# A diagonal state-space scan beside an RWKV-7 recurrence: its state tiles one by one, or in pairs side by side in the rows and columns of TensorE's array

## The chip, the core and the metric

The kernel runs on one core of a Trainium2 chip. The metric is the device time of one execution in microseconds (us). The kernel before takes 1673.89 us, the median of three runs (1672.61 to 1677.13).

## What is computed

Two layers of an encoder trunk on 256 tokens of width 1024, in float32. The even layer projects the normed tokens to two mixers, RWKV-7 time mixing (8 heads of 64) and an S5 diagonal complex state-space model (32 groups of 16 channels, 64 complex states each), and projects both outputs back; then come cross-attention to a memory of 256 tokens and a dense SwiGLU. The odd layer has differential attention, cross-attention to the same memory and 8 SwiGLU experts, two for each token. The change is in the S5 model:

```python
def s5_ssm(u, lam_re, lam_im, log_dt, b_re, b_im, c_re, c_im, d_skip, w_glu, b_glu):
    ug = u.reshape(b, t, S5_GROUPS, S5_GROUP)
    lam_bar = jnp.exp(lam * dt)
    b_bar = ((lam_bar - 1.0) / lam)[..., None] * lax.complex(b_re, b_im)
    bu = jnp.einsum('gpi,btgi->btgp', b_bar, ug)          # inputs of the states
    _, states = lax.associative_scan(combine, (lam_bar, bu), axis=1)   # x[t] = lam_bar * x[t-1] + bu[t]
    y = jnp.real(jnp.einsum('gip,btgp->btgi', c_mat, states))
    y = jax.nn.gelu(y + d_skip * ug)
    return y * jax.nn.sigmoid(y @ w_glu + b_glu)
```

## The kernel before

The 32 groups with 64 states each make 2048 complex states, which are worked on in 16 **state tiles** of 128 states on the partitions and 256 tokens along the free axis, real and imaginary part side by side (128 x 2 x 256). Tile j belongs to channel block m = j // 4 (128 channels) and to the 32 channels q = j % 4 of that block. A tile goes through three steps, which are functions in `s5_scan` (lines 546 to 609):

- `inputs(j)`: two float32 matmuls make the tile `pbu` in PSUM, one for each part. They contract over 32 channels only, so they use 32 rows of TensorE's array (rows 32q to 32q+31) and all 128 columns. VectorE multiplies `pbu` with a cosine into `xc` (L561) and with a sine into `zz` (L562), and GpSimd (POOL) adds the products (L563, L564): the states are turned by a phase table, after which the recurrence is real.
- `scan(j)`: VectorE runs the recurrence with two scan instructions (L569), one for each part, and the result is turned back: a product on VectorE (L571), one on VectorE or, for every second tile, on POOL (L574), and two POOL additions (L575, L576).
- `outputs(j)`: two matmuls that contract over the 128 states and give 32 channels, so they use all rows and 32 columns of the array (columns 32q to 32q+31). Four tiles fill one PSUM tile `py` of 128 channels; then `gelu(m)` follows.

The phase tables `tbl` (`s5_table`, lines 401 to 420) hold four tiles each; the pool has two, so tables 2 and 3 are made on the way. The pool `s5w` holds two `xc`, two `zz` and two `t1`; `ps_tr` holds two `pbu`.

The work around it: the projections of the even layer (`feat_linear`, `project`; their weights are split into two rounded halves, `wh` on ScalarE and `wl` on VectorE, L178 and L184, and multiplied in three passes, L190 to L192) from the start to 132 us; then the RWKV-7 block matrices, states and outputs (`block_matrices`, `block_states`, `block_output`: many 32x32 and 64x64 matmuls `pm`, `po`, with VectorE steps `qq`, `w`, `vt` between them), the S5 gate and the output projection. In all of this the keys and values of the memory for both layers (`memory_kv`, tiles `pf`, weights `fraw`, split on ScalarE L450 and VectorE L453) are the **filler** of TensorE. `chain()` and `pipeline()` (lines 1000 to 1044) emit the steps: each generator yields a TensorE cost and a latency, and filler goes between. The S5 tiles begin in the projections: the scheduler, which simulates the engines and takes what is ready by priority, fixes the order on each engine. Weights of this stage come through a ring of three `raw` tiles (`weight_pools(cx, 3, 2, 2)`, line 755). All loads are issued in order by one queue (SP), `raw` (L173) and `fraw` (L440) alike.

## Time and profile before

| what | value |
|---|---|
| median of three runs | 1673.89 us (1672.61 to 1677.13) |
| profiled execution | 1672.61 us, span from first to last instruction 1670.8 us |
| TensorE (PE) busy | 1619.4 us, 97% of the span |
| VectorE (DVE) busy | 639.9 us, 38% |
| ScalarE (ACT), GpSimd (POOL) busy | 476.1 us (28%), 198.5 us (12%) |
| mean granted TensorE clock | 0.976 |
| chain that ended last | PE 86%, DVE 8%, ACT 2%, POOL 2%, issue 2% |

The shares are means over stages that differ. VectorE's 38% is the mean of a first fifth in which it is busy most of the time and a rest in which it is nearly idle; the change touches that first fifth only. A granted clock of 1.00 is 2.4 GHz, 0.50 is 1.2 GHz.

### The profile page before, as it was taken

The numbers are of one execution on the slowest core, as the hardware profiler recorded it, in microseconds if no ns is written. First come the engines' busy times: TensorE is split into PE (matmuls) and PEld (weight loads), VectorE is DVE, ScalarE is ACT, GpSimd is POOL, SyncE is SP. The second block draws the span as 40 slices with busy tenths as digits, with TensorE's granted clock in tenths as the row PEclk, the third lists the DMA queues.
The fourth block names the chain that finished last, engine by engine and source line by source line (L and its number), as shares of the span: only waits on it lengthen the run. The fifth ranks groups of instructions, "written<-read, shape, count | busy, mean of one in ns | idle before, by whom it ended". The sixth has DMA issues, their size and how long they took to land.

```text
span 1670.8 us, 34308 instructions
## 1 busy us (share of the span) xinstructions
PE 1619.4 (97%) x14882; PEld 982.9 (59%) x14882; DVE 639.9 (38%) x1065; ACT 476.1 (28%) x852; POOL 198.5 (12%) x230
## 2 busy tenths in 40 slices
PE   6999999999999999999999999999999999999997
PEld 5877657899999988998334333343333433333432
DVE  7778987676555567764100011100101001010011
ACT  6466434555544456653101000010000100010000
POOL 6334473111000031110000000000000000000000
PEclk9999979999999999998999999999999999999999
DMA  6423323664555543646699889999999999999995
GB/s 227 152 89 127 109 71 115 222 255 152 186 193 180 195 156 116 239 150 239 252 387 383 333 356 407 415 418 419 419 418 418 419 419 419 418 419 387 372 419 218
DMA packets 74462, 471.48 MB, mean 282 GB/s; under 512 B 8600, under 2 KB 10008, under 8 KB 22464
## 3 DMA queue, kind: packets, MB, share of 16 engines
q1 hardware_dynamic: 73024, 465.02, 71.5%
q0 software_dynamic: 1280, 4.20, 0.7%
q8 instruction: 118, 1.93, 0.5%
q14 instruction: 40, 0.33, 0.1%
HBM read 463.94 MB, written 5.24 MB: 281 GB/s over the span
## 4 chain that ended last, share of the span: by engine, by line
PE 86%; DVE 8%; ACT 2%; POOL 2%; issue 2%; DMA 0%; SPq 0%; DVEq 0%; POOLq 0%; ACTq 0%
PE pgu L195 31%; PE pd L195 16%; PE pm L190 5%; PE pm L192 5%; PE pm L191 5%; PE pgu L190 2%; PE pgu L192 2%; PE pgu L191 2%; PE pm L195 2%; PE pgt L195 1%; PE pf L190 1%; PE pf L191 1%; PE pf L192 1%; PE po L195 1%; DVE zz L569 1%
## 5 line engine op out<-in xcount | busy, mean ns | idle before, releaser
L195 PE MATMUL pgu<-raw,gx 128*32 128x512 f32 (+1 forms) x5376 | 515.8, 542 | 0.0
L195 PEld LDWEIGHTS pgu<-raw,gx 128*32 128x32 f32 x5376 | 171.9, 110 | 319.8 <-issue 287.2
L195 PE MATMUL pd<-raw,th 128*32 128x512 f32 x2352 | 266.4, 607 | 0.4 <-DVE th L1896 0.4
L184 DVE TENSOR_TENSOR wl<-raw,wh 128x1024 fp32r<-128x1024 f32 (+1 forms) x159 | 195.0, 1238 | 103.2 <-ACT wh L178 102.8
L178 ACT ACTIVATE wh<-raw 128x1024 fp32r<-128x1024 f32 (+1 forms) x160 | 165.5, 1047 | 146.8 <-PE pgu L191 67.7
L1882 DVE SCALAR_TENSOR_TENSOR actA<-pgu,gs,actA 128x512 f32<-128x512 f32 (+1 forms) x32 | 21.9, 684 | 468.0 <-PE pgu L195 282.7
L195 PEld LDWEIGHTS pd<-raw,th 128*32 128x32 f32 x2352 | 75.5, 112 | 175.2 <-issue 171.7
L190 PE MATMUL pm<-xh,wh 128*128 128x256 f32 (+1 forms) x552 | 161.6, 296 | 14.4 <-ACT wh L178 12.4
L192 PE MATMUL pm<-xh,wl 128*128 128x256 f32 (+1 forms) x552 | 158.0, 290 | 4.9 <-DVE wl L184 4.9
L191 PE MATMUL pm<-xl,wh 128*128 128x256 f32 (+1 forms) x552 | 159.0, 289 | 2.2 <-DVE xl L1096 2.2
L1878 ACT ACTIVATE actA<-pgu,gs 128x512 f32<-128x512 f32 (+1 forms) x32 | 20.3, 634 | 448.5 <-PE pgu L195 433.5
L190 PEld LDWEIGHTS pm<-xh,wh 128*128 128x128 f32 (+1 forms) x552 | 107.6, 196 | 17.5 <-ACT wh L178 12.9
L192 PEld LDWEIGHTS pm<-xh,wl 128*128 128x128 f32 (+1 forms) x552 | 106.7, 195 | 7.1 <-DVE wl L184 6.4
L191 PEld LDWEIGHTS pm<-xl,wh 128*128 128x128 f32 (+1 forms) x552 | 107.8, 195 | 3.7 <-DVE xl L1096 2.6
L1896 DVE COPY th<-ptA 128x384 f32<-128x384 f32 (+3 forms) x32 | 14.9, 464 | 245.0 <-PE ptA L1895 245.0
L191 PE MATMUL pgu<-xl,wh 128*128 128x256 f32 x352 | 98.6, 280 | 0.0
L190 PE MATMUL pgu<-xh,wh 128*128 128x256 f32 x352 | 98.5, 280 | 0.0
L192 PE MATMUL pgu<-xh,wl 128*128 128x256 f32 x352 | 98.5, 280 | 0.0
L192 PEld LDWEIGHTS pgu<-xh,wl 128*128 128x128 f32 x352 | 66.2, 188 | 0.0
L191 PEld LDWEIGHTS pgu<-xl,wh 128*128 128x128 f32 x352 | 66.2, 188 | 0.0
L190 PEld LDWEIGHTS pgu<-xh,wh 128*128 128x128 f32 x352 | 66.1, 188 | 0.0
L453 DVE SCALAR_TENSOR_TENSOR fwl<-fraw,cols,fwh 128x512 fp32r<-128x512 f32 x64 | 56.9, 896 | 11.4 <-ACT fwh L450 11.3
(477 smaller groups left out, 2138.9 us busy)
## 6 DMA issues: line engine op xcount, KB each, us to landing
raw<-mg SPq DMA_DIRECT2D x112, 1024.0 KB, 15.5
raw<-mu SPq DMA_DIRECT2D x112, 1024.0 KB, 15.3
raw<-md SPq DMA_DIRECT2D x112, 1024.0 KB, 14.9
raw<-wgu SPq DMA_DIRECT2D x22, 1024.0 KB, 4.9
fraw<-wkv SPq DMA_DIRECT2D x32, 512.0 KB, 4.1
raw<-wqkv SPq DMA_DIRECT2D x12, 1024.0 KB, 4.9
raw<-wdn SPq DMA_DIRECT2D x11, 1024.0 KB, 4.9
raw<-hy SPq DMA_DIRECT2D x16, 512.0 KB, 3.8
```

What stands on the lines that cost most here:

```text
L178: W["act"].append(nc.scalar.activation(wh, rv, AF.Copy).ins)
L184: W["dve"].append(e_.tensor_tensor(wl[:, c_], rv[:, c_], wh[:, c_], op=ALU.subtract).ins)
L190: nc.tensor.matmul(out, lhsT=lt[0], rhs=r[0], start=start, stop=False, **kw)
L191: nc.tensor.matmul(out, lhsT=lt[0], rhs=r[1], start=False, stop=False, **kw)
L192: nc.tensor.matmul(out, lhsT=lt[1], rhs=r[0], start=False, stop=stop, **kw)
L195: nc.tensor.matmul(out, lhsT=lt, rhs=r, start=start, stop=stop, **kw)
L453: e_.scalar_tensor_tensor(wl, rv, g, wh, op0=ALU.mult, op1=ALU.subtract)
L569: nc.vector.tensor_tensor_scan(z[:, ri], rho[:, j:j + 1].to_broadcast([128, T]), xc[:, ri], 0.0, op0=ALU.mult, op1=ALU.add)
L1878: nc.scalar.activation(actA, p[0], AF.Silu, scale=gs[:, 0, 1:2])
L1882: nc.vector.scalar_tensor_tensor(actA, p[1], gs[:, 0, 1:2], actA, op0=ALU.mult, op1=ALU.mult)
L1896: nc.vector.tensor_copy(th[:, 0], ptA[:, :, 0:c])
```

## The change

The 16 state tiles become 8 pairs J = 0 to 7 (tiles 2J and 2J+1). `inputs(J)` makes both `pbu` of a pair, and its four matmuls alternate between the two tiles, which lie in different rows of the array. `outputs(J)` does the same in different columns. In the loop the scan of pair J-1 now stands ahead of the inputs of pair J, and a step is charged 1.6 us and twice the latency. The `xc` tiles move to a pool of four, `t1` to a pool of its own that is opened after the projections, and the ring of weight tiles of that stage shrinks from three to two, which pays for the room. The arithmetic is the same: as many matmuls, VectorE and POOL instructions as before.

```diff
@@ pools of the hybrid layer (line 231)
     s5t = scoped(cx, "s5t", 2)
     s5w = scoped(cx, "s5w", 2)
+    s5x = scoped(cx, "s5x", 4)
     s5 = scoped(cx, "s5", 1)
@@ s5_scan (line 546)
-        def inputs(j):
-            m, q = j // 4, j % 4
-            rows = slice(32 * q, 32 * q + 32)
-            sc = tables[m][:, q]
-            pbu = ps_tr.tile([128, 2, T], F32, name="pbu", tag="tr")
+        def inputs(J):
+            m = J // 2
+            pbu = [ps_tr.tile([128, 2, T], F32, name="pbu", tag="tr") for _ in range(2)]
             for ri in range(2):
-                mm(pbu[:, ri], sbw[rows, ri, m], uT[rows, m])
-            xc = xs[j] = s5w.tile([128, 2, T], F32, name="xc", tag="xc")
-            z = zs[j] = s5w.tile([128, 2, T], F32, name="zz", tag="zz")
-            nc.vector.tensor_tensor(xc, pbu, bc2(sc[:, 0]), op=ALU.mult)
-            nc.vector.tensor_tensor(z, pbu, bc2(sc[:, 1]), op=ALU.mult)
-            gtt(xc[:, 0], xc[:, 0], z[:, 1], op=ALU.add)
-            gtt(xc[:, 1], xc[:, 1], z[:, 0], op=ALU.subtract)
+                for i in range(2):
+                    q = 2 * (J % 2) + i
+                    rows = slice(32 * q, 32 * q + 32)
+                    mm(pbu[i][:, ri], sbw[rows, ri, m], uT[rows, m])
+            for i in range(2):
+                j = 2 * J + i
+                sc = tables[m][:, j % 4]
+                xc = xs[j] = s5x.tile([128, 2, T], F32, name="xc", tag="xc")
+                z = zs[j] = s5w.tile([128, 2, T], F32, name="zz", tag="zz")
+                nc.vector.tensor_tensor(xc, pbu[i], bc2(sc[:, 0]), op=ALU.mult)
+                nc.vector.tensor_tensor(z, pbu[i], bc2(sc[:, 1]), op=ALU.mult)
+                gtt(xc[:, 0], xc[:, 0], z[:, 1], op=ALU.add)
+                gtt(xc[:, 1], xc[:, 1], z[:, 0], op=ALU.subtract)
-        def scan(j):
+        def scan(J):
+            for j in (2 * J, 2 * J + 1):
...
-        def outputs(j):
-            m, q = j // 4, j % 4
-            if q == 0:
+        def outputs(J):
+            m = J // 2
+            if J % 2 == 0:
                 pys[m] = ps_po.tile([128, T], F32, name="py", tag="po")
-            terms = ((0, xs[j][:, 0]), (1, xs[j][:, 1]), (1, zs[j][:, 0]), (0, zs[j][:, 1]))[:4 if S5N else 2]
-            for i, (c, x) in enumerate(terms):
-                mm(pys[m][32 * q:32 * q + 32], cpad[:, c, j], x, i == 0, i == len(terms) - 1)
+            for c in range(2):
+                for i in range(2):
+                    q = 2 * (J % 2) + i
+                    mm(pys[m][32 * q:32 * q + 32], cpad[:, c, 2 * J + i], xs[2 * J + i][:, c], c == 0, c == 1)
...
-            t1 = s5w.tile([128, T], F32, name="t1", tag="t1")
+            t1 = s5g.tile([128, T], F32, name="t1", tag="t1")
...
-        for j in range(18):
-            if j > 1:
-                outputs(j - 2)
-            if j < 16:
-                inputs(j)
-            if 0 < j < 17:
-                scan(j - 1)
-            yield 1.3, S5_LAT
-            if j > 4 and j % 4 == 1:
-                gelu((j - 2) // 4)
-            if j in (5, 9):
-                s5_table(2 + j // 8)
+        for J in range(10):
+            if J > 1:
+                outputs(J - 2)
+            if 0 < J < 9:
+                scan(J - 1)
+            if J < 8:
+                inputs(J)
+            yield 1.6, 2 * S5_LAT
+            if J > 2 and J % 2:
+                gelu((J - 3) // 2)
+            if J in (2, 4):
+                s5_table(1 + J // 2)
@@ pools after the projections (line 751)
     ps_po = scoped(cx, "ps_po", 1, space=PSUM)
+    s5g = scoped(cx, "s5g", 2)
     ub = scoped(cx, "ub", 2)
-    weight_pools(cx, 3, 2, 2)
+    weight_pools(cx, 2, 2, 2)
@@ s5_gate (line 956)
-            t1 = s5w.tile([128, T], F32, name="t1", tag="t1")
+            t1 = s5g.tile([128, T], F32, name="t1", tag="t1")
```

The order on the engines at three places follows. Numbers behind a name tell buffers apart: `py_1639<-xc_1525` is an output product of the first tile. Lines of the changed kernel are a few higher than those of before (the scan is L569 before and L577 now; the products of the inputs are L561, L562 before and L568, L569 now).

TensorE at the end of the projections (132 us in the trace of before). Before:

```order
L195 MATMUL py_1639<-xc_1525,cpad_307 32x256 x2
L195 MATMUL py_1639<-xc_1576,cpad_307 32x256 x2
L764 MATMUL pt_1219<-cst_64,v_1179 128x128
L764 MATMUL pt_1225<-cst_64,v_1179 128x128
L764 MATMUL pt_1232<-cst_64,kt_1026 128x128 x4
L764 MATMUL pt_1219<-cst_64,v_1179 128x128
L764 MATMUL pt_1225<-cst_64,v_1179 128x128
L195 MATMUL pbu_1815<-uT_175,sbw_308 128x256 x2
L764 MATMUL pt_1238<-cst_64,kt_1026 128x128 x4
L195 MATMUL pbu_1902<-uT_175,sbw_308 128x256 x2
```

and now (the four output products of pair 0, in the same order, stand ahead of these):

```order
L195 MATMUL py_1708<-xc_1628,cpad_310 32x256
L195 MATMUL py_1708<-xc_1634,cpad_310 32x256
L195 MATMUL py_1708<-xc_1628,cpad_310 32x256
L195 MATMUL py_1708<-xc_1634,cpad_310 32x256
L770 MATMUL pt_1225<-cst_64,v_1182 128x128
L770 MATMUL pt_1231<-cst_64,v_1182 128x128
L770 MATMUL pt_1238<-cst_64,kt_1029 128x128 x4
L770 MATMUL pt_1225<-cst_64,v_1182 128x128
L770 MATMUL pt_1231<-cst_64,v_1182 128x128
L195 MATMUL pbu_1880<-uT_178,sbw_311 128x256 x2
L770 MATMUL pt_1244<-cst_64,kt_1029 128x128 x4
L195 MATMUL pbu_1881<-uT_178,sbw_311 128x256 x2
```

Before, the outputs of tiles 0 and 1 stand here, two matmuls of one tile and then two of the other, and the inputs of tiles 4 and 5, each alone. Now the outputs of four tiles stand here, alternating in pairs, and the inputs of pair 3 (tiles 6 and 7), which transposes keep apart.

TensorE among the 32x32 blocks of the RWKV-7 recurrence. Before (tile 8) and now (pair 6):

```order
L195 MATMUL pm_2483<-w_1725,aa_1429 32x32 x13
L195 MATMUL py_2462<-xc_2217,cpad_307 32x256
L195 MATMUL pm_2483<-w_1725,aa_1429 32x32 x8
L195 MATMUL py_2462<-xc_2217,cpad_307 32x256
L195 MATMUL pm_2483<-w_1725,aa_1429 32x32 x11
L195 MATMUL pm_2524<-w_1767,aa_1470 32x32 x32
```

```order
L195 MATMUL py_2604<-xc_2323,cpad_310 32x256
L195 MATMUL pm_2628<-w_1797,aa_1476 32x32 x25
L195 MATMUL py_2604<-xc_2329,cpad_310 32x256
L195 MATMUL py_2604<-xc_2323,cpad_310 32x256
L195 MATMUL pm_2628<-w_1797,aa_1476 32x32 x7
L195 MATMUL pm_2674<-qq_1748,vt_1747 32x32 x7
L195 MATMUL py_2604<-xc_2329,cpad_310 32x256
L195 MATMUL pm_2674<-qq_1748,vt_1747 32x32 x25
```

Both kernels have output products here one by one between the small blocks. Of pair 6 the middle two, one of each tile, stand together.

VectorE around `zm`, the result of the low-rank projection (51.9 us in the trace of before). Before, and now:

```order
L571 TENSOR_TENSOR xc<-zz,tbl 128x512
L569 SCALAR_TENSOR_TENSOR zz<-s5c_302,xc 128x256 x2
L474 TENSOR_SCALAR mem<-mem,rs 128x1024
L574 TENSOR_TENSOR zz<-zz,tbl 128x512
L571 TENSOR_TENSOR xc<-zz,tbl 128x512
L184 TENSOR_TENSOR wl<-raw,wh 128x1024
L617 TENSOR_TENSOR zm<-pm,rsB_149 128x2x256
L618 TENSOR_TENSOR zm<-pm,rsB_149 32x256
```

```order
L577 SCALAR_TENSOR_TENSOR zz<-s5c_305,xc 128x256 x2
L568 TENSOR_TENSOR xc<-pbu,tbl 128x512
L577 SCALAR_TENSOR_TENSOR zz<-s5c_305,xc 128x256 x2
L568 TENSOR_TENSOR xc<-pbu,tbl 128x512
L579 TENSOR_TENSOR xc<-zz,tbl 128x512 x2
L184 TENSOR_TENSOR wl<-raw,wh 128x1024
L581 TENSOR_TENSOR zz<-zz,tbl 128x512
L622 TENSOR_TENSOR zm<-pm,rsB_152 128x2x256
L623 TENSOR_TENSOR zm<-pm,rsB_152 32x256
```

Ahead of `zm` there are now two more products `xc<-pbu` (L568), those of pair 1; the products `zz<-pbu` and the scans of pair 1, and the third phase table, follow behind `zm`, in the projections, where before they stood behind the last projection.

## Rows read from the trace of the kernel before

**Rows 1.** The page of the whole execution: its first line, the and the busy time of each engine.
```profile
span 1670.8 us, 34308 instructions
...
PE 1619.4 (97%) x14882; PEld 982.9 (59%) x14882; DVE 639.9 (38%) x1065; ACT 476.1 (28%) x852; POOL 198.5 (12%) x230
```

**Rows 2.** Busy time of each engine by stage, from the first input product to the end of the output projection. Columns: stretch in us, its length, busy us and instructions of PE, PEld, DVE, ACT and POOL, granted TensorE clock, DMA share, GB/s.
```profile
37.00:60.00 23.00, 20.44 (x141) 17.72 (x140) 21.11 (x32) 9.65 (x16) 16.26 (x20) 0.93 0.44 138
60.00:100.00 40.00, 40.00 (x248) 33.54 (x247) 22.01 (x33) 23.55 (x44) 5.95 (x8) 1.00 0.47 152
100.00:135.00 35.00, 31.40 (x189) 26.13 (x188) 28.11 (x38) 18.64 (x42) 11.20 (x9) 0.90 0.35 116
135.00:224.00 89.00, 85.25 (x1485) 57.19 (x1483) 82.96 (x138) 44.02 (x73) 44.97 (x48) 0.98 0.34 107
224.00:241.30 17.30, 16.41 (x291) 9.99 (x291) 15.56 (x25) 6.26 (x16) 13.92 (x18) 0.51 0.05 19
241.30:270.00 28.70, 26.21 (x221) 17.34 (x220) 20.95 (x29) 11.05 (x24) 17.72 (x18) 0.94 0.35 120
270.00:345.00 75.00, 75.00 (x556) 66.61 (x554) 53.75 (x84) 41.93 (x67) 14.77 (x20) 1.00 0.57 207
```

**Rows 3.** The chain that ended last, of the stretch 132 to 262 us alone, by engine and line.
```profile
by line: DVE zz L569 12.3%; issue 11.2%; DVE fwl L453 9.8%; DVE zz L562 5.2%; PE pm L195 5.0%; DVE xc L571 4.8%; PE py L195 4.3%; DVE xc L561 4.3%; POOL xc L564 3.4%; POOL xc L576 2.7%; DVE wl L184 2.6%; POOL xc L563 2.6%; PE pf L190 2.6%; 
```

**Rows 4.** TensorE's instructions in order of time: start in us, from the first start to the last end, line, tiles, shapes, how many of one kind stand together (a float32 matmul is two instructions), and the idle time ahead with what ended it. First two input products together and what comes next, at 38 us.
```profile
37.91 1.14 PE L195 MATMUL pbu<-uT,sbw 32*128 32x256 f32 x8
38.98 0.31 PE L190 MATMUL pm<-xh,wh 128*32 128x256 f32 x1
```

**Rows 5.** The same view from 131 to 150 us: output products of two tiles, input products of one tile, two products of the same tile apart or of two tiles together.
```profile
132.00 1.06 PE L195 MATMUL py<-xc,cpad 128*32 128x256 f32 x8
133.00 0.44 PE L764 MATMUL pt<-cst,v 128*128 128x128 f32 x2
...
134.43 1.13 PE L195 MATMUL pbu<-uT,sbw 32*128 32x256 f32 x4 [0.34 <-DVE zz L562]
135.49 0.66 PE L764 MATMUL pt<-cst,kt 128*128 128x128 f32 x4
...
148.08 0.62 PE L195 MATMUL py<-xc,cpad 128*32 128x256 f32 x2
148.63 0.74 PE L190 MATMUL pf<-fwh,mth 128*128 128x512 f32 x2
149.29 0.63 PE L195 MATMUL py<-xc,cpad 128*32 128x256 f32 x4
149.85 0.34 PE L195 MATMUL pm<-bt,ar 64*64 64x64 f32 x4
```

**Rows 6.** The same view at 182 us (both products of one tile) and at 230 us (single products).
```profile
182.02 1.05 PE L195 MATMUL py<-xc,cpad 128*32 128x256 f32 x4
183.00 1.13 PE L195 MATMUL pbu<-uT,sbw 32*128 32x256 f32 x4
...
230.51 1.22 PE L195 MATMUL pbu<-uT,sbw 32*128 32x256 f32 x2
231.66 0.31 PE L195 MATMUL pm<-qq,vt 32*32 32x32 f32 x2
231.90 1.06 PE L195 MATMUL py<-xc,cpad 128*32 128x256 f32 x2
232.89 0.33 PE L195 MATMUL pm<-qq,vt 32*32 32x32 f32 x8
```

**Rows 7.** Groups of instructions by line and shape, 130 to 270 us. Columns: line, engine, operation, out<-in, shapes, how many | busy us, mean ns of one | idle us of the engine ahead of them, and what ended it.
```profile
L453 DVE SCALAR_TENSOR_TENSOR fwl<-fraw,cols,fwh 128x512 fp32r<-128x512 f32 x32 | 30.5, 952 | 3.9 <-ACT fwh L450 3.8
...
L569 DVE TENSOR_TENSOR_SCAN zz<-s5c,xc 128x256 f32<-128x256 f32 x28 | 24.3, 906 | 2.8 <-POOL xc L564 2.8
...
L195 PE MATMUL py<-xc,cpad 128*32 128x256 f32 x64 | 19.0, 425 | 3.5 <-POOL xc L575 3.0 <-POOL xc L576 0.5
L195 PE MATMUL pbu<-uT,sbw 32*128 32x256 f32 x48 | 14.8, 425 | 1.2 <-DVE zz L562 1.2
...
L571 DVE TENSOR_TENSOR xc<-zz,tbl 128x512 f32<-128x512 f32 x14 | 11.6, 829 | 0.1
...
L561 DVE TENSOR_TENSOR xc<-pbu,tbl 128x512 f32<-128x512 f32 x14 | 9.5, 680 | 4.3 <-POOL bv L933 2.4 <-PE pbu L195 1.3 <-PE py L195 0.6
...
L411 DVE TENSOR_SCALAR tbl<-cst,s5c 128x256 f32<-128x256 f32 x8 | 4.6, 631 | 0.0
...
L414 DVE SCALAR_TENSOR_TENSOR tbl<-cst,s5c,tbl 128x256 f32<-128x256 f32 x8 | 3.6, 476 | 0.0
...
L413 DVE SCALAR_TENSOR_TENSOR tbl<-tbl 128x256 f32<-128x256 f32 x8 | 2.9, 413 | 0.0
```

**Rows 8.** TensorE in order of time (the columns of Rows 4), where the low-rank projection is done and the key projection begins.
```profile
52.73 0.36 PE L190 MATMUL pm<-xh,wh 128*128 128x256 f32 x1 [1.94 <-DVE zm L617]
```

**Rows 9.** Who waited for whom, 130 to 270 us: engine, line, releaser: us in total, times, longest.
```profile
PE py L195 <- POOL xc L575: 3.0, 3, 1.5
...
PE pbu L195 <- DVE zz L562: 1.2, 2, 0.9
```

**Rows 10.** The load queue's own waits (SP), 100 to 330 us, in the same columns.
```profile
SPq L440 <- DVE fwl L453: 141.1, 20, 22.8
SPq L173 <- DVE wl L184: 17.5, 2, 12.5
```

16 lines of the change are left out of this document (6 added, 10 removed).

## The prediction

> **What bounds the kernel now.** I read the page first: TensorE (PE) is busy 97% of 1670.8 us [rows 1], so a change pays only where it takes time off PE or off a wait of PE. Then the stages [rows 2]: from 135 to 270 us, where nearly all of the S5 work lies, PE is busy 85.25 of 89, 16.41 of 17.3 and 26.21 of 28.7 us, so it idles 7.1 us in 135; VectorE (DVE) is nearly as full, 82.96 of the first 89. From 270 to 345 us PE is busy without a gap. The filler, the products of the memory's keys and values, is what keeps PE full: its amount is fixed, so what PE saves before 345 us lets the rest come earlier, as long as DVE and the weights follow. The chain of waits between 132 and 262 us [rows 3] is mostly DVE's: scans, splits of filler weights, S5 products. So there are two bounds close together, PE's sum and DVE's chain, and the change touches both. Last, what one product costs on PE [rows 4 to 6] and who waits for whom [rows 9, 10].
>
> **What side by side is worth.** The trace of before has the paired form in it. Four input products of two tiles (eight instructions) start at 37.91 and the next thing at 38.98: 1.07 us [rows 4]. Two of one tile take 134.43 to 135.49: 1.06 us [rows 5]. Two tiles cost what one does. For outputs the same: 132.00 to 133.00 for two tiles [rows 5], 182.02 to 183.00 for one [rows 6]. Single output products cost 148.08 to 148.63 = 0.55 us, and one of each of two tiles together 0.56 [rows 5]. I take 0.55 for a single input product as well.
>
> *Inputs.* Before, one pair stands together, 13 tiles stand whole but alone, one tile in two places: 1.07 + 13 x 1.06 + 2 x 0.55 = 15.95 us. In the changed order pairs 0, 2, 5, 6, 7 stand together (5 x 1.07), pairs 3 and 4 are kept apart (4 x 1.06), and of pair 1 one product stands alone, three together (0.55 + 1.06): 11.2 us. **-4.75 us.**
>
> *Outputs.* Before: one pair together (1.00), tiles 2 and 3 in three places (1.65), tiles 4 to 7, 12 and 13 whole (6 x 0.98), tiles 8 to 11, 14 and 15 in two places each (12 x 0.55): 15.1 us. Now: pairs 0 and 1 in one run (2 x 1.0; 1.0 if four columns run at once), pair 2 one alone and three together (0.55 + 0.98), pairs 3, 4, 5 together (3 x 1.0), pairs 6 and 7 in three places each (6 x 0.55): 9.8 us. **-5.3 us.** The rows of the groups say 14.8 and 19.0 us busy [rows 7], more than these sums, as they hold tails that overlap and pieces at the lower clock.
>
> That two products of one tile followed by two of the other run side by side (the run at 132.00 [rows 5], which the order shows so) means that standing together decides, not the alternation inside the pair. The Trainium skill speaks against this (TensorE: Matmul & The Clock Gate, Part 3: packing small matmuls): matmuls start and end strictly in program order, so that only the alternating order would overlap. By that rule pair 2's inputs, which the changed order still has two and two, would cost 2.1 us, and the sum would be 1 us smaller; the trace does not agree, and I go by the trace.
>
> **What moves.** Ahead of `zm` DVE now has two more input products. `zm` is what PE waits 1.94 us for at 52.73 [rows 8]; two products at 0.68 us (L561 [rows 7]) make that wait longer: **+1.4 us** (0 if they fit into DVE's other waits there, 3 if POOL's additions, on which the scans in between wait, come late too).
>
> Behind `zm`, the rest of pair 1 and the third phase table move from after 132 us into the projections: two products `zz` (1.36), four scans at 0.7 to 0.9 (3.2), three turn-back products (2.2), table 4 x 0.63 + 4 x 0.41 + 4 x 0.48 (6.1), some 12.9 us of DVE [rows 7]. What hides them: between 60 and 100 us DVE is busy 22 of 40 us, POOL 6 [rows 2]. I cost them at nothing; if the splits `wl` stand behind a scan that waits for POOL, PE, which is full there, loses the wait. In exchange DVE, which was full from 135 to 224, has 12.9 us less to do there. That is why I let PE's saving come through whole.
>
> The scan of pair J-1 now stands ahead of the inputs of pair J, and there are two `zz` tiles: inputs can only begin when POOL has finished with the pair before. PE's waits for S5 were 3.5 us for POOL before an output and 1.2 us for DVE before an input [rows 7, 9], 4.7 us of its 7.1. A pair apart, an output follows its last addition by a whole step, which makes such waits rarer; a pair's run is longer, which makes them longer. I leave them as they are: 0, from -4.7 to +4.
>
> The weight ring of three becomes two. SP stood 17.5 us in two waits for a `wl` to free a ring tile [rows 10]; PE had filler meanwhile. I take 0, with +12.5 (one more wait of the longest length, uncovered) as the end.
>
> The clock: from 224 to 241.3 us the granted clock is 0.51, the 1.2 GHz level, though PE is busy 16.41 us [rows 2]; a single product there takes 1.15 or 0.99 us [rows 6] against 0.55. Small 32x32 blocks and single S5 products fill PE ahead of it and in it, and they still stand there in the new order. I leave the stretch as it is: 0, from -6 to +6 (half of 16.41 would be 8.2; the small blocks lose less).
>
> **Sum.** -4.75 - 5.3 + 1.4 = -8.7 us. Against the profiled execution of 1672.61 us, which is 1.3 us below the median of 1673.89, that is 1663.9, **1664.0 us**. What comes after 345 us is moved earlier as a whole. Its own range, with the smaller ends above, is 1658 to 1669.
>
> **Rivals.**
>
> 1. *More than the sum* (1653 us). With outputs a step behind their additions the 4.7 us of waits go, and without the single products the stretch at 1.2 GHz goes too, another 6 us: 1664 - 4.7 - 6 = 1653. For it: pf products stand between the small blocks more evenly in the new order. Against it: pairs 6 and 7 are still given out singly among the blocks. Chance 0.13.
>
> 2. *DVE is the bound and PE's saving turns into waits* (1674 us). DVE is as full as PE from 135 to 224 us; the change takes no instruction from it, and a scan whose neighbour on POOL is busy takes 0.91 us in the mean [rows 7]. PE then waits for splits of filler weights where it had S5 products. Price: the 10 us back, the 1.4 us stays: 1674. Against it: 12.9 us of DVE leave this stretch. By the Trainium skill (SBUF — State Buffer, SBUF: two separate sides) VectorE with two inputs in SBUF and GpSimd shut each other out for a whole instruction, which would lengthen DVE where pairs put more POOL work beside it; no row here separates that. Chance 0.17.
>
> 3. *The ring of two holds the load queue, and the filler runs dry: slower* (1683 us). SP issues in order: a `raw` load that waits for its ring tile holds every `fraw` load behind it, and without `fraw` there is no filler. Before, two loads waited, 12.5 us at the longest [rows 10]; a ring of two makes at least one load more wait. It decides from the point where the wait outlasts the filler whose weights have landed. Price: one to two waits of 12.5 us uncovered, 1676 to 1689, 1683 taken. For it: `fraw` loads already stand 141 us in waits [rows 10]. Against it: the scheduler put the later output weights further back in SP's queue. Chance 0.12.
>
> The change doing less than it says (pairs that don't stand together) is in the sum already, from the order.
>
> **How the numbers follow.** A difference under about 0.3%, 5 us, cannot be told from none here. My sum has 0.58: 0.53 below 1668.9, 0.05 in the band; rival 1 0.13, faster; rival 2 0.17, 0.15 in the band and 0.02 above; rival 3 0.12, 0.11 above and 0.01 in the band. Faster 0.66, same 0.21, slower 0.13. The range runs from rival 1 to the lower half of rival 3, 1652 to 1678; some 0.06 lies below it and 0.12 above.
>
> **What would show it.** Right: input and output products in runs of eight instructions of about 1.07 us, their busy time together down from 33.8 us [rows 7] by a third or more in the stretch that answers to 130 to 270; the wait for `zm` near 3.3 us; the output projection's end, and all that follows, about 9 us earlier; PE still without a gap after it. Wrong: PE waits for `wl` or `wh` between 57 and 100 us; waits of `pf` products for `fwl` or for loads that grow by 5 us or more (rival 2 or 3); SP waits of `raw` for `wl` well above 17.5 us; or the granted clock at 0.5 over a stretch much longer or shorter than 17 us.

## Result: slower by 0.9%, and the profile after

The changed kernel takes 1689.36 us in the median of four runs (1683.86 to 1689.7) against 1673.25 us for the kernel before, a ratio of 1.0093 with a 95% interval of 1.0069 to 1.0116. The forecast was 1664.0 us, range 1652 to 1678: wrong in sign. The profiled execution of the changed kernel took 1683.86 us, the fastest of its four, 11.3 us more than that of before.

The page of the changed kernel answers to [rows 1]:

```profile
span 1682.1 us, 34324 instructions
...
PE 1612.7 (96%) x14882; PEld 989.7 (59%) x14882; DVE 638.3 (38%) x1065; ACT 475.8 (28%) x852; POOL 208.6 (12%) x230
```

PE is busy 6.7 us *less*, while the span grew by 11.3 us. Taken apart, the S5 products need 14.3 us less of PE (shown below), its other products, as many as before, 7.6 us more, and PE's idle time grew by 18.0 us: -14.3 + 7.6 + 18.0 = 11.3. The mean granted clock of the whole execution is 0.971 for 0.976, which goes with the 7.6 us. POOL is busy 10 us more with the same instructions. The same seven stretches as in [rows 2], in the same columns:

```profile
37.00:60.00 23.00, 18.92 (x123) 16.61 (x122) 21.00 (x31) 7.30 (x14) 15.77 (x21) 0.85 0.43 138
60.00:100.00 40.00, 36.66 (x243) 33.01 (x243) 33.48 (x55) 25.69 (x40) 20.91 (x15) 0.96 0.42 133
100.00:135.00 35.00, 33.08 (x160) 24.18 (x159) 24.86 (x31) 21.24 (x45) 12.33 (x10) 0.90 0.23 75
135.00:224.00 89.00, 82.31 (x1303) 58.96 (x1302) 78.52 (x130) 39.30 (x70) 46.76 (x51) 0.88 0.33 108
224.00:241.30 17.30, 13.38 (x353) 8.41 (x351) 16.15 (x26) 2.89 (x4) 13.34 (x13) 0.90 0.40 124
241.30:270.00 28.70, 25.10 (x382) 20.28 (x382) 13.42 (x22) 13.77 (x33) 10.46 (x17) 0.88 0.19 60
270.00:345.00 75.00, 68.51 (x441) 56.49 (x441) 41.94 (x69) 33.17 (x58) 10.92 (x14) 0.93 0.43 146
```

Three places lose. From 60 to 100 us, where PE was full, it idles 3.3 us; DVE has 33.48 us of work there for 22.01 and POOL 20.91 for 5.95. From 135 to 241.3 us PE idles 10.6 us for 4.6. From 241.3 to 345 us, where PE had no gap after 270, it idles 10.1 us for 2.5 and the clock is 0.88 and 0.93. The stretch of 17 us at clock 0.51 is gone (0.90), which the prediction had in rival 1 alone; in exchange 135 to 224 fell from 0.98 to 0.88.

**The products side by side.** TensorE in order of time, the columns of [rows 4]: pair 2's inputs at 64 us, then the first outputs and inputs of the S5 stage.

```profile
64.62 1.14 PE L195 MATMUL pbu<-uT,sbw 32*128 32x256 f32 x8
65.69 0.50 PE L191 MATMUL pf<-fwl,mth 128*128 128x512 f32 x1
```

```profile
140.10 1.08 PE L195 MATMUL py<-xc,cpad 128*32 128x256 f32 x16
141.12 0.44 PE L770 MATMUL pt<-cst,v 128*128 128x128 f32 x2
...
142.54 1.12 PE L195 MATMUL pbu<-uT,sbw 32*128 32x256 f32 x4 [0.33 <-DVE zz L569]
143.59 0.66 PE L770 MATMUL pt<-cst,kt 128*128 128x128 f32 x4
```

Eight input instructions take 1.07 us as before [rows 4]; the prediction's other reading had 2.1 us for this pair. Sixteen output instructions, four tiles in four column groups, take 1.02 us to the next start, about as long as eight or four did [rows 5, 6]: four run side by side. The groups of 130 to 270 us that answer to [rows 7]:

```profile
L454 DVE SCALAR_TENSOR_TENSOR fwl<-fraw,cols,fwh 128x512 fp32r<-128x512 f32 x31 | 29.5, 963 | 7.1 <-ACT fwh L451 7.1
...
L577 DVE TENSOR_TENSOR_SCAN zz<-s5c,xc 128x256 f32<-128x256 f32 x24 | 19.1, 827 | 0.1
...
L195 PE MATMUL py<-xc,cpad 128*32 128x256 f32 x64 | 10.8, 422 | 4.2 <-POOL xc L582 4.2
...
L195 PE MATMUL pbu<-uT,sbw 32*128 32x256 f32 x40 | 7.9, 400 | 0.3 <-DVE zz L569 0.3
```

Outputs fell from 19.0 to 10.8 us. Over the whole stretch from 30 to 350 us outputs and inputs together fell from 37.1 to 22.8 us: 14.3 us saved where 10 were forecast. The pairing does what it is meant to do; the loss lies elsewhere.

**The projections.** VectorE in order of time from 67 to 83 us; the columns are start, duration, engine, line, operation, tiles, count and the idle time ahead.

```profile
67.73 1.27 DVE L577 TENSOR_TENSOR_SCAN zz<-s5c,xc 128x256 f32<-128x256 f32 x2 [0.64 <-POOL z L627]
...
69.10 0.67 DVE L579 TENSOR_TENSOR xc<-zz,tbl 128x512 f32<-128x512 f32 x1
...
70.37 0.67 DVE L579 TENSOR_TENSOR xc<-zz,tbl 128x512 f32<-128x512 f32 x1
70.97 0.67 DVE L581 TENSOR_TENSOR zz<-zz,tbl 128x512 f32<-128x512 f32 x1
...
73.49 3.05 DVE L412 TENSOR_SCALAR tbl<-cst,s5c 128x256 f32<-128x256 f32 x4 [1.19 <-POOL zz L581]
76.47 1.08 DVE L414 SCALAR_TENSOR_TENSOR tbl<-tbl 128x256 f32<-128x256 f32 x3
77.47 0.87 DVE L415 SCALAR_TENSOR_TENSOR tbl<-cst,s5c,tbl 128x256 f32<-128x256 f32 x2
78.26 0.68 DVE L631 TENSOR_TENSOR z<-pm,rsB 128x512 f32<-128x512 f32 x1
...
80.73 0.68 DVE L631 TENSOR_TENSOR z<-pm,rsB 128x512 f32<-128x512 f32 x1
...
83.12 0.87 DVE L643 SCALAR_TENSOR_TENSOR k<-z,omu,k 128x256 f32<-128x256 f32 x2
```

The same place before:

```profile
68.15 1.23 DVE L184 TENSOR_TENSOR wl<-raw,wh 128x1024 fp32r<-128x1024 f32 x1 [1.83 <-ACT wh L178]
69.31 1.40 DVE L626 TENSOR_TENSOR z<-pm,rsB 128x512 f32<-128x512 f32 x2
...
72.13 1.66 DVE L638 SCALAR_TENSOR_TENSOR k<-z,omu,k 128x256 f32<-128x256 f32 x4
```

The key projection's `z` (L626 before, L631 now) is taken out of PSUM at 78.26 and 80.73 for 69.31 us, and `k` begins at 83.12 for 72.13. In front of it stand pair 1's scans and turn-back products and the third phase table; the table's first instruction (73.49) itself waited 1.19 us for POOL's `zz`, since a table tile is free only when pair 1 has read it. TensorE was through with the projection's products at 73.46 us, so `z` lay ready for 4.8 us behind the table in VectorE's order: it waited for a buffer that it has nothing to do with. ScalarE waits 5.6 us for the same `zz` ahead of its part of the table, with a weight split `wh` behind it. TensorE's waits from 36 to 100 us (engine, line, releaser: us in total, times, longest), the first three:

```profile
PE pm L190 <- DVE zm L622: 2.7, 1, 2.7
PE pm L190 <- DVE z L631: 2.6, 1, 2.6
PE pbu L195 <- DVE zz L569: 1.3, 1, 1.3
...
```

`zm` [rows 8] costs 0.8 us more; `z`, not waited for before, 2.6; pair 1's input products wait 1.3 us for pair 0 to leave `pbu`. The first output product comes at 140.10 us for 132.00 [rows 5]. From the start to it, before and now:

```profile
0.00:132.00 132.00, 110.07 (x674) 95.83 (x674) 94.37 (x156) 74.81 (x137) 56.61 (x83) 0.94 0.49 160
```

```profile
0.00:140.10 140.10, 114.17 (x682) 98.25 (x682) 107.47 (x179) 81.44 (x146) 74.55 (x93) 0.91 0.44 145
```

Of the 8.1 us, 4.0 are idle time of PE. The other 4.1 are busy time: 1.1 for pair 2's inputs (eight instructions more), and some 3 because the same products take longer at a mean clock of 0.91 for 0.94. The filler does not fill the delay: 96 of its products stand ahead of the first output in both kernels.

**The S5 stage.** TensorE's waits from the first output product to the next stage (140 to 361 us):

```profile
PE ptf L509 <- ACT kx L505: 4.9, 1, 4.9
PE py L195 <- POOL xc L582: 4.2, 3, 3.0
PE pm L195 <- DVE qq L829: 3.9, 1, 3.9
PE pm L190 <- ACT xh L952: 2.0, 1, 2.0
PE pm L195 <- DVE a L807: 1.9, 1, 1.9
...
```

Apart from `xc`, which is S5's own, they are waits for steps of the *other* chains: the block matrices (`qq`, `a`), the S5 gate (`xh`), the normed keys of the filler (`kx`). S5's last output product ends at 243.5 us for 266.8. Of PE's 20.7 us of idle time in this stage, 10.9 lie ahead of that point (7.5 before) and 9.8 behind it, where PE had no gap before.

### The profile page after: what moved, and what is told of

It reads as the page before. It is cut to its first block, busy times and chain, and to the rows that moved or that the text cites. A ratio compares the mean times of both kernels' runs of the same rounds, so it can differ in the third digit from the quotient of the medians.

```text
span 1682.1 us, 34324 instructions
## 1 busy us (share of the span) xinstructions
PE 1612.7 (96%) x14882; PEld 989.7 (59%) x14882; DVE 638.3 (38%) x1065; ACT 475.8 (28%) x852; POOL 208.6 (12%) x230
## 4 chain that ended last, share of the span: by engine, by line
PE 82%; DVE 8%; POOL 3%; DMA 3%; ACT 2%; issue 2%; SPq 0%; DVEq 0%; POOLq 0%; ACTq 0%
PE pgu L195 29%; PE pd L195 15%; PE pm L190 5%; PE pm L192 5%; PE pm L191 5%; PE pgu L190 2%; PE pgu L191 2%; PE pgu L192 2%; PE pm L195 2%; PE pf L190 2%; PE pf L191 1%; PE pf L192 1%; PE po L195 1%; DMA raw<-mu 1%; DVE zz L577 1%
## 5 line engine op out<-in xcount | busy, mean ns | idle before, releaser
L195 PEld LDWEIGHTS pgu<-raw,gx 128*32 128x32 f32 x5376 | 175.6, 110 | 316.4 <-issue 282.2
L195 PE MATMUL pd<-raw,th 128*32 128x512 f32 x2352 | 262.6, 599 | 0.4 <-DVE th L1902 0.4
L1888 DVE SCALAR_TENSOR_TENSOR actA<-pgu,gs,actA 128x512 f32<-128x512 f32 (+1 forms) x32 | 21.9, 684 | 468.9 <-PE pgu L195 283.5
## 6 DMA issues: line engine op xcount, KB each, us to landing
raw<-mg SPq DMA_DIRECT2D x112, 1024.0 KB, 17.4
raw<-mu SPq DMA_DIRECT2D x112, 1024.0 KB, 16.4
```

The costliest lines, as they stand in the source:

```text
L195: nc.tensor.matmul(out, lhsT=lt, rhs=r, start=start, stop=stop, **kw)
L1888: nc.vector.scalar_tensor_tensor(actA, p[1], gs[:, 0, 1:2], actA, op0=ALU.mult, op1=ALU.mult)
```

## Experiments

Positions of all runs, from their traces in us: the first output product `py`; the first mask `arb` of the block matrices on VectorE; the end of VectorE's last `yt` product, a step near the end of the block matrices (ScalarE's last copy into `yt` ends 5 to 18 us later: at 252.0 us before, at 253.6 in the changed kernel); the end of the last `py`; the first product of the next stage (`ssp`); and PE's idle time between first `py` and next stage (length less busy, by stretches as in [rows 2]). The ratio is to the kernel before on the same chip. Positions and idle times are of one execution each. e12 and e18 are the same kernel on two chips, and PE is busy 196.5 us in the one and 200.0 in the other (idle 16.4 and 13.1), so differences of 3 us in the last column tell little.

| run | ratio, 95% interval | first py | arb | last yt | last py | next stage | PE idle |
|---|---|---|---|---|---|---|---|
| before | 1 | 132.0 | 146.2 | 239.8 | 266.8 | 347.3 | 7.5 |
| changed | 1.0093 (1.0069 to 1.0116) | 140.1 | 156.2 | 248.3 | 243.5 | 361.0 | 20.7 |
| e1_hold | 1.0040 (1.0015 to 1.0066) | 133.8 | 158.7 | 250.3 | 240.3 | 354.0 | 23.8 |
| e2_pools | 1.0119 (1.0082 to 1.0155) | 145.3 | 161.5 | 254.3 | 276.6 | 366.2 | 18.0 |
| e3_ring2 | 1.0003 (0.9989 to 1.0018) | 132.9 | 147.0 | 240.7 | 267.7 | 348.9 | 7.9 |
| e4_pace | 1.0054 (1.0035 to 1.0073) | 142.1 | 158.2 | 260.1 | 250.8 | 356.8 | 18.3 |
| e5_hold_pace | 1.0021 (1.0007 to 1.0035) | 134.0 | 158.4 | 255.0 | 241.0 | 353.4 | 20.7 |
| e6_holdtable | 1.0176 (1.0152 to 1.0199) | 136.6 | 154.0 | 256.3 | 251.5 | 375.0 | 30.0 |
| e7_scanfirst | 0.9995 (0.9978 to 1.0012) | 131.7 | 145.8 | 239.5 | 266.5 | 347.0 | 7.5 |
| e8_hold_pace_act | 1.0018 (1.0004 to 1.0033) | 134.4 | 160.1 | 254.9 | 239.3 | 353.4 | 23.9 |
| e9_pools_hold | 1.0017 (0.9997 to 1.0037) | 133.9 | 159.0 | 244.5 | 267.2 | 354.8 | 16.2 |
| e10_hold_arb | 1.0091 (1.0070 to 1.0112) | 133.8 | 143.4 | 261.2 | 259.2 | 364.8 | 17.4 |
| e11_half_steps | 1.0044 (1.0026 to 1.0062) | 134.0 | 158.9 | 246.6 | 268.2 | 357.4 | 29.8 |
| e12_latency | 0.9985 (0.9975 to 0.9994) | 132.6 | 157.5 | 231.7 | 261.7 | 345.5 | 16.4 |
| e13_lat_single | 1.0109 (1.0078 to 1.0140) | 131.4 | 157.2 | 228.9 | 281.4 | 359.6 | 18.0 |
| e14_lat_before | 1.0082 (1.0053 to 1.0112) | 132.9 | 147.1 | 225.2 | 290.3 | 354.9 | 15.4 |
| e15_lat_act | 1.0029 (1.0011 to 1.0046) | 134.9 | 160.6 | 238.2 | 268.1 | 349.5 | 21.9 |
| e16_latency8 | 1.0146 (1.0115 to 1.0176) | 132.3 | 157.5 | 224.5 | 287.5 | 363.7 | 20.8 |
| e17_arb_early | 1.0057 (1.0042 to 1.0073) | 134.4 | 150.3 | 237.1 | 277.1 | 360.2 | 23.7 |
| e18_latency_again | 0.9995 (0.9979 to 1.0010) | 133.1 | 158.1 | 232.6 | 262.4 | 346.2 | 13.1 |

### Which part of the change costs (e1 to e4, e7)

**e1_hold.** `behind` makes the instructions of its function follow a given split of the projections' weights on VectorE and ScalarE.

```diff
-                inputs(J)
+                behind(len(W["dve"]) - 1 if J == 1 else -1, lambda: inputs(J))
```

> The changed kernel with one thing taken back: pair 1's inputs (and with them its scan and the third phase table) may not start on VectorE before the last split of the projections' weights; so from 60 to 130 us S5 is again as it was before the change. Theory 1 (the four xc buffers let pair 1 and the table into the projections, where they stand ahead of z and wl on VectorE): the first output product returns from 140 to about 132 us, PE's waits for z and zm fall to under 2 us, and about 8 us of the 16 come back: 1681 us. If PE's saving in the S5 stage then comes through as well, 1672. Theory 2 (the loss lies in the S5 stage itself, where pair-long runs of VectorE and GpSimd hold up the other chains): the first output product comes earlier, but the 13 us of VectorE work that now lie in the S5 stage cost as much there: 1686 to 1692, no change against the changed kernel. Theory 3 (the weight ring of two): no change, 1689.

Measured 1677.9 us: 11.5 us of the 16 came back by the medians, 9 by the ratios. VectorE is as it was from 60 to 100 us:

```profile
60.00:100.00 40.00, 40.00 (x253) 33.75 (x252) 23.13 (x35) 24.07 (x44) 5.82 (x8) 1.00 0.46 152
```

Theory 1 holds for the projections: the first output product is back at 133.8 us and PE no longer waits for `z`, though its wait for `zm` stayed, at 3.1 us, against what I expected. That the 14 us of PE come through as well does not hold: the S5 stage still takes 220.2 us for 215.3, with PE idle 23.8 of them. Of these, 18.5 lie ahead of S5's last output product, and 7.5 are waits for splits of filler weights (`fwl`, `fwh`), 2.0 before.

**e2_pools.** The kernel before with `xc` from `s5x` of four, `t1` from `s5g`, `weight_pools(cx, 2, 2, 2)`; loop and products untouched.

> The kernel before, tile by tile as it was, with the changed kernel's pools alone: four xc buffers, t1 in a pool of its own, and the weight ring of the later stage of two for three. No pairing, scan and inputs in the old order. Theory 1: four buffers alone let tiles 2 and 3 and the third table into the projections, so the first output product comes at about 140 us for 132 and the kernel loses about 8 us: 1681 us. Theory 2 (pairing and scan first are what costs): the same as before within 0.3%, 1673. Theory 3 (ring): 1679 or more, but then the kernel with the ring of two alone loses the same.

1691.08 us: the pools alone cost all that the change costs. (The ring is taken out by e3 below; the pool of `t1` was not tried by itself.) The first output product comes at 145.3 us, and the row of 60 to 100 us shows why:

```profile
60.00:100.00 40.00, 35.90 (x240) 32.53 (x238) 29.97 (x52) 23.72 (x36) 17.93 (x16) 0.96 0.40 132
```

Before, inputs of tile 2 could not start until an output product had freed one of two `xc` tiles, and outputs need a PSUM tile that is opened only behind the projections. The pool of two was what held S5 back. With four, the scheduler puts tiles 2 and 3 and the third table where it finds VectorE free, in front of `z`.

**e3_ring2.** The kernel before with the weight ring of two alone.

```diff
-    weight_pools(cx, 3, 2, 2)
+    weight_pools(cx, 2, 2, 2)
```

> The kernel before with the weight ring of the later stage of two for three, nothing else. Theory 3: raw loads wait for wl longer, fraw loads behind them come late, and 6 us or more are lost: 1680. Theories 1 and 2: the same as before within 0.3%, 1673.

1673.0 us, no change: theory 3 falls, and with it rival 3 of the prediction.

**e4_pace.** `yield 2.6, 2 * S5_LAT` for `yield 1.6, 2 * S5_LAT`.

> The changed kernel with one number: a pair's step counts 2.6 us of PE in the planner's account for 1.6, as two tiles did before. Theory 4 (pacing: S5 is given out too early, it ends 23 us earlier than before, and the later stage lacks its work): the last output product comes at 250 us or later for 243, and 4 to 6 us come back: 1684. Theories 1 to 3: within 0.3% of the changed kernel, 1689.

1681.47 us, 7.9 us better by the medians and 6.5 by the ratios, a little more than theory 4 had, and the last output product at 250.8 us; PE's wait for `kx`, 4.9 us, is under 1 and the mean granted clock of the stage is 0.94 for 0.91. So a part of the loss in the changed order is how early S5 is given out.

**e7_scanfirst.** The kernel before with `scan(j - 1)` moved ahead of `inputs(j)`.

> The kernel before, tile by tile and with its own pools, with one thing of the change: the scan of the tile before stands ahead of the next tile's inputs. If scan first by itself costs (inputs now wait for GpSimd's last addition of the tile before, and the load of VectorE comes in longer pieces): 1676 to 1682. If it is free: 1673 within 0.3%. If it gains, because outputs wait less for GpSimd (3.0 us of PE's waits in the stage before): 1669 to 1671.

1672.0 us: scan first is free, tile by tile.

### Where the saving goes (e5, e6, e8 to e11)

**e5_hold_pace.** e1's and e4's edits together.

> The changed kernel with pair 1's inputs held behind the projections (as in the first run) and a pair's step counted at 2.6 us of PE (as in the fourth). The two took 11.5 and 7.9 us off the changed kernel's 1689.4 apart. Theory A (two separate losses, one in the projections, one in the S5 stage, where S5 runs ahead of the other chains): they add, 1670, the same as before or a little faster; the first output product at 134 us, PE's idle time from there to the next stage, 23.8 us in the first run, falls to 15 or less. Theory B (VectorE is the bound of the S5 stage, however it is paced): 1676 to 1678, as the first run, since the held work and the paced work queue for the same engine.

1676.7 us: they do not add, as theory B had it. Its reason, VectorE's sum, was to be tested next.

**e8_hold_pace_act.** e5 with `TA = 'vvaa'` for `'vvvv'`.

> The fifth run's kernel (pair 1 held, a pair counted at 2.6 us) with one thing more: the first of the three products of each row of phase tables 3 and 4 runs on ScalarE for VectorE, which takes 8 instructions of 0.63 us, 5.0 us, off VectorE in the S5 stage; ScalarE is busy under two thirds there. Theory B (VectorE is the bound of the stage): 3 to 5 us faster than the fifth run. Theory A (the order of the chains, not VectorE's sum, sets the stage): within 1.5 us of the fifth run.

1675.63 us, within 1.1 us. By theory A VectorE's sum would then not be the bound, but the edit did not take 5 us off VectorE. The eight instructions that moved are 3.2 us in e5; of those that stayed, L414 takes 6.0 us for 2.8, and from 30 to 360 us VectorE is busy 255.5 us for 256.6. Up to S5's last output product VectorE is nearly full in e5:

```profile
134.00:241.00 107.00, 89.55 (x1498) 59.08 (x1500) 102.89 (x165) 48.86 (x85) 67.08 (x74) 0.91 0.32 105
```

It is busy 96% of that stretch here and in e1, 97% in e8, for 89% up to the same point in the kernel before and in the changed one. So theory B stays open for these orders.

**e6_holdtable.** The changed kernel with only the table behind the projections.

```diff
-                s5_table(1 + J // 2)
+                behind(len(W["dve"]) - 1 if J == 2 else -1, lambda: s5_table(1 + J // 2))
```

> The changed kernel with the third phase table alone held behind the projections' last split; pair 1's inputs and scan stay in the projections. If the table is what makes z late (four phase products of 0.63 us, eight others, and additions on GpSimd beside them, right ahead of z on VectorE): first output product at 133 to 135 us for 140, and 6 us or more of the loss come back, 1683. If pair 1's scans and products do it: first output product at 138 or later, 1687 to 1689. If it is the sum of both: half each.

In the projections it gave 3.5 of the 8.1 us back (first `py` at 136.6), so the table is nearly half of that delay. The time went the other way, 1702.22 us: PE idles 30.0 us in the stage at a mean clock of 0.87. Its longest waits are 6.9 us for a split `wh` of the output projection and 3.9 for `qq`; why the order fell out so badly I did not separate.

**e9_pools_hold.** e2 with tiles 2 and 3 held: e5 without the pairing.

```diff
-                inputs(j)
+                behind(len(W["dve"]) - 1 if j in (2, 3) else -1, lambda: inputs(j))
```

> The second run's kernel (tile by tile as before the change, with the changed kernel's pools) with tiles 2 and 3 held behind the projections' last split, as pair 1 was in the first run. It is the fifth run's kernel without the pairing: its distance to that run (1676.7) is what the pairing is worth by itself. If pairing gives PE's 14 us and nothing takes them back: 1688 to 1691 here. If the S5 stage is not bound by PE, so that the saving goes into waits: 1675 to 1679 here, within 0.2% of the fifth run, with the first output product at 134 us and some 14 us more of py and pbu on PE for some 14 us less of idle time. If the pools cost only through the projections: 1673, as before the change.

1675.24 us against e5's 1676.7: at this pacing pairing is worth nothing. The stage's busy time of e5 and of e9 from the first output product to the next stage (columns of [rows 2]):

```profile
134.00:353.40 219.40, 198.74 (x2573) 151.15 (x2572) 173.44 (x280) 107.04 (x189) 88.78 (x101) 0.94 0.40 139
```

```profile
133.90:354.80 220.90, 204.65 (x2576) 155.41 (x2575) 175.35 (x279) 106.36 (x189) 89.50 (x101) 0.94 0.42 148
```

Pairing takes 5.9 us off PE's busy time and idle time takes 4.4 of them. In e5 S5 is through at 241.0 and VectorE's last `yt` product at 255.0; in e9 it is the other way round, 267.2 and 244.5. So with the pairs S5 came through earlier and the block matrices later. That this is why the saving does not arrive is not shown.

**e10_hold_arb.** e5 with pair 1's scan and pair 2's inputs behind `arb`; the lines that differ from the changed kernel, cut.

```diff
-            if 0 < J < 9:
-                scan(J - 1)
-            if J < 8:
-                inputs(J)
...
+            with tc.issue_after(W["arb"][-1]) if J == 2 else ExitStack():
+                if 0 < J < 9:
+                    scan(J - 1)
+                if J < 8:
+                    behind(len(W["dve"]) - 1 if J == 1 else -1, lambda: inputs(J))
```

> The fifth run's kernel with pair 1's scan and pair 2's inputs held on VectorE behind the four masks arb of the block matrices. In the fifth run pair 1, the third table and pair 2's products stand ahead of arb in VectorE's order, arb starts at 158 us for 146 before the change, and the chain of block matrices ends at 249 to 254 for 231 to 239. Theory A1 (four xc buffers let S5 run ahead a second time, here in front of the block matrices, and that chain is what the stage waits for): arb at 147 to 150, the block matrices' end 6 us or more earlier, 1669 to 1672. If the chain of S5 is as late as that of the block matrices (VectorE is full): within 2 us of 1676.7, the loss moved to S5's outputs.

`arb` came at 143.4 us, and the time was 1689.45: PE waited 10.2 us for S5's `xc`, and the last `yt` product came later (261.2), not earlier. Theory A1 in this form falls.

**e11_half_steps.** e5 with a pair's VectorE work in two steps; a pair's input products stand ahead of the scans again. The lines of the loop, against the changed kernel:

```diff
-            if 0 < J < 9:
-                scan(J - 1)
-            if J < 8:
-                inputs(J)
-            yield 1.6, 2 * S5_LAT
+            pbu = inputs(J) if J < 8 else None
+            for i in range(2):
+                if 0 < J < 9:
+                    scan(J - 1, i)
+                if J < 8:
+                    behind(len(W["dve"]) - 1 if J == 1 else -1, lambda: turn(J, i, pbu[i]))
+                yield 1.3, S5_LAT
```

> The fifth run's kernel with a pair's VectorE work given out in two steps of 1.3 us, tile by tile, each with its own latency, while the matrix products stay in pairs. Theory 2 (what takes the saving back are pair-long runs of VectorE and GpSimd in front of the other chains' short steps): PE's waits for qq and w fall from about 7 us to 3 or less, 1671 to 1673. If the length of a step does not matter: within 1.5 us of 1676.7.

1681.92 us, and PE's wait for `qq` rose to 10.9 us: theory 2 in this form falls as well.

### Pacing, and what pairing is worth (e12 to e18)

**e12_latency.** e5 with `yield 2.6, 5 * S5_LAT`.

> The fifth run's kernel with a pair's latency in the planner's account at 10 us for 4: S5 is given out more slowly, over the whole stage, and the block matrices' steps stand ahead of more of it. If S5 given out too early is what is left of the loss: the last output product at 255 us or later for 240, the block matrices' end at 240 for 249 to 254, 1670 to 1673. If not: 1676 or slower, because S5's end becomes the late one.

1670.59 us: the last `yt` product ends at 231.7 us and the last output product at 261.7, PE's waits for VectorE's `qq`, 3.4 us in e5, are gone, and behind S5's end PE idles 0.8 us.

**e13_lat_single.** e9 with `yield 1.3, 2.5 * S5_LAT`: e12 without the pairing.

> The twelfth run's kernel without the pairing: the ninth run's (tile by tile, the changed pools, tiles 2 and 3 held) with 5 us of latency for each tile, 10 for two. The twelfth took 1670.6. If the pairing's 14 us on PE come through once the pacing is right: 1680 or more here. If the pairing is worth little even then, because the stage is bound by the chains on VectorE and not by PE's sum: 1669 to 1674, and PE's idle time from the first output product to the next stage is about 14 us shorter than in the twelfth run while its busy time is as much longer.

1685.89 us. Here S5 is the late chain (281.4 us), and at this pacing pairing is worth 1.2% (0.9985 against 1.0109). But this pacing does not suit single tiles: at theirs they take 1.0017 (e9), and against that the pairs are ahead by 0.2 to 0.3% (0.9985 in e12, 0.9995 in e18), which the intervals do not set apart with certainty. The two stages, with pairs and without:

```profile
132.60:345.50 212.90, 196.50 (x2577) 150.76 (x2575) 173.62 (x273) 105.84 (x188) 89.71 (x101) 0.94 0.40 140
```

```profile
131.40:359.60 228.20, 210.20 (x2573) 160.53 (x2572) 176.63 (x274) 106.55 (x188) 89.91 (x102) 0.90 0.39 139
```

PE is busy 13.7 us less with the pairs (`py` and `pbu` 8.2 of it, 27.1 for 35.3; the clock, 0.94 for 0.90, is in it too), and idle time does not grow. The planner's account is not quite the same in both, 10 steps of 10 us against 18 of 5, so some of the 15 us may be pacing.

**e14_lat_before.** The kernel before with `yield 1.3, 2.5 * S5_LAT`.

> The kernel before, with its own pools, and one number: 5 us of latency for each tile for 2. If what the twelfth run gained over the fifth (6.1 us) is to be had by pacing alone, without the change: 1666 to 1670. If the kernel before is already paced by its two xc buffers, which let S5 go no further ahead than one tile: the same, 1671 to 1674, or slower, with S5's end the late one.

1681.48 us, 0.8% slower, with S5's end at 290.3: the kernel before gains nothing from slower pacing.

**e15_lat_act.** e12 with `TA = 'vvaa'`.

> The twelfth run's kernel with the first product of each row of phase tables 3 and 4 on ScalarE for VectorE: 8 instructions of 0.63 us, 5 us less on VectorE. The same edit gave 1 us on the fifth run's kernel, within its uncertainty. If VectorE's sum bounds the stage once the order is right: 1666 to 1668. If not: 1669.5 to 1672, and then neither PE's sum nor VectorE's is the bound, but waits from one chain's step to the next.

1674.23 us, 3.6 us more than e12 by the medians and 7.3 by the ratios. Here VectorE did become 5.1 us less busy (256.8 for 261.9 from 30 to 360 us), so in e12's order its sum is not the bound. `arb` moved from 157.5 to 160.6 us and S5's end from 261.7 to 268.1.

**e16_latency8.** e12 with `yield 2.6, 8 * S5_LAT`.

> The twelfth run's kernel with 16 us of latency for a pair for 10. In the twelfth run the block matrices end at 226 to 231 us and S5's last output product at 261. If S5 is already late enough there: S5's end moves to 268 or later, the S5 gate after it, and the time is 1671 to 1676. If the block matrices are still what the stage waits for: 1667 to 1669.

1691.63 us, worse than the 1671 to 1676 that the first case gave, with S5's end at 287.5 as it had it.

**e17_arb_early** and **e18_latency_again.** e17 is e12 with pair 2's inputs and the third table, but not pair 1's scan, behind `arb`; e18 is e12 once more.

```diff
-                behind(len(W["dve"]) - 1 if J == 1 else -1, lambda: inputs(J))
+                with tc.issue_after(W["arb"][-1]) if J == 2 else ExitStack():
+                    behind(len(W["dve"]) - 1 if J == 1 else -1, lambda: inputs(J))
...
-                s5_table(1 + J // 2)
+                with tc.issue_after(W["arb"][-1]) if J == 2 else ExitStack():
+                    s5_table(1 + J // 2)
```

> The twelfth run's kernel (pair 1 held behind the projections, a pair counted at 2.6 us with 10 us of latency) with pair 2's inputs and the third phase table held on VectorE behind the masks arb, but pair 1's scan left ahead of them, as in the order of before. In the twelfth run arb starts at 157 us for 146 before the change. If S5's lead in front of arb is part of what still eats the pairing's saving: arb at 148 to 151, the block matrices' end 5 us earlier, S5's end no later than 265, 1664 to 1668. If not, because S5's end becomes the late one (as in the sixteenth run): last output product at 268 or later, 1671 to 1676.

> The twelfth run's kernel once more, on the same chip as the seventeenth and with more rounds, to see whether its gain over the kernel before (ratio 0.9985, interval 0.9975 to 0.9994) stands: 0.997 to 1.0.

e17, of which the first case was expected at 1664 to 1668: `arb` at 150.3 us as wanted, but S5's end at 277.1, as the second case had it, and 1681.99 us, above the range of either. e18: 0.9995 (0.9979 to 1.0010), so e12's lead over the kernel before is not confirmed; mended, the change is even with it. What stays open is whether an order exists in which the saving comes through whole: with both mends PE is busy 11.3 us less than before in the stage (196.5 for 207.8) and idle 8.9 us more (e12's trace). Against the run that each changes, slower or finer pacing (e11, e12, e16) moved the last `yt` product forward and S5's end back; the two edits that took `arb` forward (e10, e17) put both back.

## Why the prediction was wrong

- *Products side by side*: right in kind, low in size. I took 10.05 us; 14.3 were measured. Most of the difference is in the sum for before: 31.05 us by single durations, 37.1 in the trace (now 21.0 and 22.8). Four column groups run at once (sixteen instructions in 1.02 us), which I had in brackets only; that is 1 us of it.
- *`zm`*: +1.4 forecast, 0.8 measured as PE's wait.
- *The 12.9 us behind `zm`, "I cost them at nothing"*: this step failed. The cover that I named, DVE busy 22 of 40 us, is a sum; what counted was what stands next in VectorE's order behind the moved work, `z`, and that the moved work itself waits, for POOL and for table tiles. I wrote as a sign of being wrong that PE would wait for `wl` or `wh`; it waited for `z` (2.6 us) and hardly for `wl` (0.5), and the first output product came 8.1 us late. e1 and e2 show the step: the pools alone delay the first output product by 13.3 us, and holding pair 1 brings it back to within 1.8 and takes 0.5% of the 0.9% away. I read the move in the order and did not see what caused it, a buffer count that had worked as a brake.
- *"That is why I let PE's saving come through whole"*: failed too, and by itself. With pair 1 held (e1) PE still idles 23.8 us in the stage, for 7.5. VectorE has 15.3 us less to do in the stage (163.2 for 178.5), so the premise came true, and still PE's idle time there went from 7.5 to 20.7 us. Rival 2 named the outcome, PE's saving turned into waits (the 0.91 us that it gives for a scan beside a busy POOL is the mean of all 28 scans). Whether its cause, VectorE's sum, is the right one stays open: in e1 and e5 VectorE is 96% busy until S5's end, in the changed kernel 89%, and only e12's order is shown not to hang on it (e15). What the runs do show is that pacing decides: the charge of 1.6 us for a pair, which I did not price, is part of it (e4), and with pair 1 held and a pair's latency at 10 us the loss is gone (e12, e18). It is not simply the later of two ends: S5's last output product came 23 us earlier and the last `yt` product 8.5 us later, so that the later of the two moved from 266.8 to 248.3 us, while the next stage began 13.7 us later.
- *PE's waits for S5 left as they are*: near in size, 4.2 + 0.3 us in the S5 stage for 4.7, and 1.3 in the projections.
- *The ring, rival 3*: 0 taken, 0 measured (e3). It was my only way to a slower kernel; the true one was another.
- *The clock left as it is*: too small. The stretch of 17 us at the lower level went, and others came, in the projections too (0.85 for 0.93 from 37 to 60 us): mean granted clock of the S5 stage 0.91 for 0.94. PE's products outside S5 took 7.6 us more in all; the end of +6 that I gave was for the one stretch. The clock fell where PE idled more (e6 0.87 with 30.0 us idle, e16 0.88 with 20.8), but not in e8 (0.95 with 23.9), so idle time alone does not tell it.
- *The sum*: it starts from the profiled execution of 1672.61 us; from the median of 1673.89 it gives 1665.2, which changes nothing here.

## What to carry to other kernels

A pool's size is also a brake on how far a scheduler runs one chain ahead: when a change adds buffers, look in the order of every in-order engine for what then moves in front of whose work, and price the work behind it, not the engine's free time. A saving on one engine's sum arrives only if that engine has other work ready in its new gaps; where several chains share a stage, look at where its idle time lies before counting the saving, and let pacing numbers follow a new step size. Take a change apart by its enablers too: the pools alone cost as much here as the whole change.
